# Which engine waits for the last stores and clears their semaphore: GpSimd in place of SyncE

## The chip, the cores and the metric

The kernel runs on one core of one Trainium2 chip. A core has five engines with an instruction stream each: TensorE (not used here), VectorE (DVE in the profile), ScalarE (ACT), GpSimd (POOL) and SyncE (SP, which only issues transfers and handles semaphores). They run in parallel and order their work by semaphores: an instruction may wait until a semaphore has reached a value, and may raise one when it is done. The metric is the device time of one execution in microseconds (us).

## The reference

The input has shape (32, 512, 1024) in float32. For each of the 16,384 rows of 1024 numbers the variance is wanted, as mean of squares less square of the mean:

```python
def reference(x: np.ndarray) -> np.ndarray:
    mean_sq = np.mean(x**2, axis=-1)
    sq_mean = np.mean(x, axis=-1)**2
    return (mean_sq - sq_mean).astype(np.float32)
```

So 64 MiB are read and 64 KiB are written.

## The kernel before

The 16,384 rows are laid out as 128 partitions by 128 columns; a column is one row of 1024 numbers on each partition. The results gather in the tile `mv`, whose second half `mv[:, 1, :]` is what is stored.

SyncE issues all transfers, one after the other. Two buffers `xt0` and `xt1` hold 16 columns each. They are filled and emptied in three turns (96 columns), and the last 32 columns come in eight loads of falling size (`END_LOADS`) and three pieces of one column (`PIECES`), so that little work is left when the last bytes land. `load` (L97) issues a transfer, with a semaphore that rises by 16 when it has landed.

The work on the columns is shared. VectorE takes `BATCH_NORM_STATS2` and an aggregate for most of them (L121, L223 in a loop, L253 to L276 at the end). ScalarE takes the others in two passes, a mean and then squares about it (L125, L130), and one half of the last column but one (L306, L312). GpSimd copies finished results into `mv` (L176) and joins the statistics of 14 of VectorE's columns (L184 to L203); its last instruction is the third L203.

What stands around the change is the end of SyncE's program, L332 to L343. Three stores go out, each from `store` (L106, issued at L108) and each raising `stored` by 16 when it has landed. The first, of 16 columns, waits for the first copy (L332). The second waits for GpSimd's last step, for ScalarE and for VectorE (L334 to L336). The third waits for VectorE's last aggregate, L276 (L338). Then SyncE waits until VectorE has raised `ended` five times (L278, L279, L340) and clears the semaphores of the list `sems` with one instruction (L341). `stored` isn't in that list. For it SyncE waits until it has reached 48, that is until all three stores have landed, and clears it by a second instruction (L342, L343). A wait and the instruction behind it appear as one instruction in the profile.

`sync` is SyncE and `gps` is GpSimd (L82).

Of the kernel before, what the change touches and what calls it, by code (L numbers as in the profile page):

```python
# [11 lines left out]
def kernel(  # L12
# [69 lines left out]
    sync, act, dve, gps = nc.sync, nc.scalar, nc.vector, nc.gpsimd  # L82
# [11 lines left out]
    stored = nc.alloc_semaphore("stored")  # L94
# [244 lines left out]
    store(early, ncols)  # L339
    sync.wait_ge(ended, DVE_END)  # L340
    sync.sem_clear(range(sems[0].num, sems[-1].num + 1))  # L341
    sync.wait_ge(stored, 48)  # L342
    sync.sem_clear(stored)  # L343


# [28 lines left out]
```

## Time and profile before

| what | value |
|---|---|
| median of 3 runs | 162.6 us (162.5 to 162.6) |
| the profiled execution's own time | 162.62 us |
| its span, first to last instruction | 161.3 us |
| VectorE busy | 103.3 us (64%) |
| ScalarE busy | 106.1 us (66%) |
| GpSimd busy | 4.1 us (3%) |
| read from memory | 67.11 MB, 416 GB/s over the span |
| third store, from issue to landing | 1.4 us |

The span runs from the first to the last instruction of the program; what the time has beyond it lies before and behind. The chain of work that ended last is followed back from the last instruction, at each step to what released it. In a row of a waits view stand who waited, for whom, the total in us, how often, and the longest. In a row of one line's view stand engine and operation, the count, the shortest, median and longest duration in ns, and the first and last start in us. A "q" behind an engine's name means that its sequencer did it, the part that waits, branches and issues. Beside the instructions, the trace records each time that a semaphore's value was changed, with the semaphore's number, also after the last instruction of the program.

### The profile page before, as it was taken

The page shows a single profiled execution, that of the slowest core. Times are in us where ns is not written, and L with a number is a line of the kernel's source. Part 1 is how long each engine was busy: PE and PEld are TensorE (multiplying, and loading weights), DVE is VectorE, ACT ScalarE, POOL GpSimd, SP SyncE. Part 2 cuts the span into 40 slices and gives each one's busy share as a digit, 9 for nine tenths or more (in the row PEclk, how much of TensorE's full clock was granted, in tenths as well). Part 3 has the DMA queues.
Part 4 walks back from the last instruction along what each step waited for, and adds up shares of the span by engine and source line. Part 5 has one row for each costly group of instructions (what it writes and reads, how often), then busy time and mean ns, then how long its engine had stood idle before and what let it go on. Part 6 is the DMA issues. An engine that isn't in the chain of part 4 may idle for free. (4 is left out here: it accounts for less than half of the span.)

```text
span 161.3 us, 577 instructions
## 1 busy us (share of the span) xinstructions
DVE 103.3 (64%) x232; ACT 106.1 (66%) x189; POOL 4.1 (3%) x20
## 2 busy tenths in 40 slices
DVE  0000029980499606994089921999139999999896
ACT  3000039972599807996089941999339979999994
POOL 0000000000000000000000000000000000000700
DMA  7969969959959959959959969969969999899993
GB/s 264 520 260 520 520 260 520 520 260 520 520 260 520 520 260 520 520 260 520 520 260 520 520 276 504 520 276 504 520 260 504 406 390 496 360 441 412 425 396 89
DMA packets 2883, 67.20 MB, mean 417 GB/s; under 512 B 704, under 2 KB 960, under 8 KB 1344
## 3 DMA queue, kind: packets, MB, share of 16 engines
q1 hardware_dynamic: 2880, 67.18, 97.3%
q14 instruction: 3, 0.02, 0.1%
HBM read 67.11 MB, written 0.07 MB: 416 GB/s over the span
## 5 line engine op out<-in xcount | busy, mean ns | idle before, releaser
L121 DVE BATCH_NORM_STATS2 stats<-xt 128x6 f32<-128x512 f32 x120 | 71.8, 680 | 54.9 <-DVEq L117 54.9
L125 ACT ACTIVATE junk<-xt 128x1024 bf16<-128x1024 f32 x41 | 42.7, 1043 | 44.1 <-ACTq L117 43.7
L130 ACT ACTIVATE junk_sq<-xt,neg_mean 128x1024 f32<-128x1024 f32 x36 | 39.9, 1107 | 5.6 <-ACTq L117 4.1
L121 DVE BATCH_NORM_STATS2 stats_join<-xt 128x6 f32<-128x512 f32 x22 | 13.1, 684 | 0.0
L125 ACT ACTIVATION_READ_ACCUMULATOR junk<-xt 128x1 f32 x41 | 7.7, 187 | 0.0
L130 ACT ACTIVATION_READ_ACCUMULATOR junk_sq<-xt,neg_mean 128x1 f32 x36 | 6.7, 186 | 0.0
L223 DVE BATCH_NORM_AGGREGATE stage<-stats 128x2 f32<-128x12 f32 x60 | 5.1, 163 | 0.9
L130 ACT ACTIVATE junk_sq<-xt_end,neg_mean_end 128x1024 f32<-128x1024 f32 x5 | 5.5, 1110 | 0.1
L130 ACT ACTIVATE junk_sq<-xt,neg_mean_end 128x1024 f32<-128x1024 f32 x5 | 5.5, 1105 | 0.1
L125 ACT ACTIVATE junk<-xt_end 128x1024 bf16<-128x1024 f32 x5 | 5.2, 1044 | 0.2 <-DMA xt_end<-in_x_dram 0.2
L253 DVE BATCH_NORM_STATS2 stats_end<-xt_end 128x6 f32<-128x512 f32 x6 | 4.1, 685 | 0.7 <-DMA xt_end<-in_x_dram 0.7
L176 POOL COPY mv<-stage 128x32 f32<-128x32 f32 x3 | 0.6, 209 | 130.9 <-ACT junk_sq L130 130.9
L257 DVE BATCH_NORM_STATS2 stats_end<-xt_end 128x6 f32<-128x512 f32 x6 | 3.9, 647 | 0.0
L121 DVE BATCH_NORM_STATS2 stats_join<-xt_end 128x6 f32<-128x512 f32 x6 | 3.7, 696 | 0.0
L281 ACT ACT_TABLE_LOAD x1 | 1.3, 1283 | 2.8 <-PEq L156 2.8
L269 DVE BATCH_NORM_STATS2 stats_end<-xt_end 128x6 f32<-128x256 f32 (+1 forms) x3 | 1.3, 490 | 0.0
L262 DVE BATCH_NORM_AGGREGATE mv<-stats_end 128x2 f32<-128x12 f32 x6 | 1.2, 194 | 0.0
L130 ACT ACTIVATION_READ_ACCUMULATOR junk_sq<-xt,neg_mean_end 128x1 f32 x5 | 0.9, 187 | 0.0
L125 ACT ACTIVATION_READ_ACCUMULATOR junk<-xt_end 128x1 f32 x5 | 0.9, 186 | 0.0
L130 ACT ACTIVATION_READ_ACCUMULATOR junk_sq<-xt_end,neg_mean_end 128x1 f32 x5 | 0.9, 186 | 0.0
L312 ACT ACTIVATE junk_sq<-xt_end,shared 128x512 f32<-128x512 f32 x1 | 0.7, 691 | 0.1
L306 ACT ACTIVATE junk<-xt_end 128x512 bf16<-128x512 f32 x1 | 0.6, 630 | 0.1
(20 smaller groups left out, 5.1 us busy)
## 6 DMA issues: line engine op xcount, KB each, us to landing
xt<-in_x_dram SPq DMA_DIRECT2D x2, 4096.0 KB, 19.1
xt_end<-in_x_dram SPq DMA_DIRECT2D x1, 2560.0 KB, 29.4
xt_end<-in_x_dram SPq DMA_DIRECT2D x1, 2048.0 KB, 33.8
xt_end<-in_x_dram SPq DMA_DIRECT2D x2, 1024.0 KB, 36.8
xt_end<-in_x_dram SPq DMA_DIRECT2D x2, 512.0 KB, 39.0
xt_end<-in_x_dram SPq DMA_DIRECT2D x1, 256.0 KB, 39.6
xt_end<-in_x_dram SPq DMA_DIRECT2D x2, 128.0 KB, 36.0
xt<-in_x_dram SPq DMA_DIRECT2D x6, 24.1
```

Of the source, the lines that this page charges most:

```text
L121: last = dve.bn_stats(out=st[:, h, :], in_=xcol[:, h * H : (h + 1) * H])
L125: return act.activation(out=junk[i], in_=xcol, func=ACTF.Copy, scale=-S / D, accum_out=nm)
L130: return act.activation(out=junk_sq[i], in_=xcol, func=ACTF.Square, scale=S, bias=nm, accum_out=var)
L176: gps.tensor_copy(out=mv[:, 1, t * PER_TURN : (t + 1) * PER_TURN], in_=stage[:, :, 1]).then_inc(copied, 1)
L223: last = dve.bn_aggr(out=stage[:, j, :], in_=stats[:, j, :, :])
L253: dve.bn_stats(out=st[:, 0, :], in_=col[:, :H])
L257: dve.bn_stats(out=st[:, 1, :], in_=col[:, H:]).then_inc(dve_step, 1)
L262: return dve.bn_aggr(out=mv[:, :, c], in_=st)
L269: last = dve.bn_stats(out=st[:, i, :], in_=end_col(c)[:, f : f + size])
L281: act.preload_act_table(ACTF.Square)
L306: act.activation(out=junk[0][:, :H], in_=half, func=ACTF.Copy, scale=1.0 / H, accum_out=shared[:, 0, 1:2],).then_inc(act_step, 1)
L312: act.activation(out=junk_sq[0][:, :H], in_=half, func=ACTF.Square, scale=-1.0, bias=shared[:, 0, 1:2], accum_out=shared[:, 0, 2:3],).then ...
```

## The change

The wait for `stored` and its clearing are given to GpSimd. They come after all else in the text of the program, so on GpSimd they stand behind the last L203. SyncE's program ends with L341.

```diff
     store(early, ncols)
     sync.wait_ge(ended, DVE_END)
     sync.sem_clear(range(sems[0].num, sems[-1].num + 1))
-    sync.wait_ge(stored, 48)
-    sync.sem_clear(stored)
+    gps.wait_ge(stored, 48)
+    gps.sem_clear(stored)
```

## The prediction

> **What bounds the kernel now.** I read the chain of work that ended last, then SyncE's waits, then the rows of the two lines that the change moves, and last the trace's record of semaphore changes, which goes on behind the last instruction. The chain first:
>
> ```profile
> ## 4 chain that ended last, share of the span: by engine, by line
> DMA 21%; DVE 6%; ACT 1%; SPq 1%; issue 0%
> ```
>
> The kernel is bound by the load of 67 MB and then by the statistics of the last columns. VectorE finishes these at 159.81 us, and after that no engine computes. The change touches only what comes after. SyncE's waits show that part:
>
> ```profile
> SPq L108 <- DVE mv L276: 4.7, 1, 4.7
> SPq L343 <- DMA out_dram<-mv: 1.0, 1, 1.0
> ```
>
> The last store is issued when the last aggregate is done, and L343 waits 1.0 us for it to land. The rows of L341 and L343 (duration, start, start):
>
> ```profile
> L341 SPq EVENT_SEMAPHORE_RANGE_CLEAR  x1: 68/68/68, 160.2 to 160.2; - x1
> ...
> L343 SPq EVENT_SEMAPHORE_RANGE_CLEAR  x1: 25/25/25, 161.3 to 161.3; - x1
> ```
>
> L343 is the last instruction of the span. The issue row gives the store's flight, and GpSimd's timeline its last work:
>
> ```profile
> out_dram<-mv SPq DMA_DIRECT2D x1, 3.5 KB, 1.4
> ```
>
> ```profile
> 152.58 0.87 POOL L203 TENSOR_SCALAR mv<-mu 128x6 f32<-128x6 f32 x3
> ```
>
> GpSimd has been done since 153.45 us, so it can stand at a wait 7.8 us ahead of the landing.
>
> The semaphore record tells what follows. The store's last landing is at 161.265 us, and L343 starts at 161.281, clears its semaphore and ends at 161.306. Semaphore 2, which the kernel doesn't use, then changes in a pattern. Its nine changes at the end of this program are at 2.968, 159.261, 159.299, 160.699, 161.438, 161.481, 161.519, 161.554 and 161.600 us. I match them with the engines' last instructions: TensorE's is at 2.68, ScalarE's busy time ends at 159.14, GpSimd's at 153.45, VectorE's last increment starts at 159.96, and SyncE's clear ends at 161.306. So each engine reports when it is done and its predecessor has reported, in the order TensorE, ScalarE, GpSimd, VectorE, SyncE. GpSimd, long done, follows ScalarE by 38 ns. Then the pass goes back through VectorE, GpSimd, ScalarE and TensorE. SyncE is last now, and **from its report to the end of the pass takes 162 ns**. After the pass, from 161.559 on, the semaphores change once more in five blocks of neighbouring numbers. The block that ends last (up to 53) starts after the 161.600 change and ends at 162.165. A second nine-step pass runs from 162.389 to 162.746. The profiled execution took 162.62 us with a span of 161.3, so some 1.3 us lie outside, about as long as this closing from 161.306 to 162.746. The median of the runs shown is 162.6 (162.5 to 162.6), so the profiled one stands for them.
>
> **The change, part by part.** *Removed from SyncE*: one wait and one clear. SyncE is then free at L341's end, 160.29 us, and waits for VectorE's report at 160.70. Nothing that SyncE issues moves: its three stores, with the same waits, stand ahead of both lines, on the same queue. The landing stays at 161.265. The gain is the whole tail between landing and SyncE's report, 161.438 - 161.265 = 173 ns, and it counts only if nothing takes its place.
>
> *Added to GpSimd*: the same wait and the same clear behind L203. Nothing of the kernel is queued behind them on GpSimd, and no instruction waits for them. What waits is the closing pass: VectorE, SyncE and the way back can't go on until GpSimd has reported. No data moves, and no other queue is passed.
>
> The price of GpSimd's tail, from landing to report, by its own rows at the start of the program:
>
> ```profile
> L156 POOLq EVENT_SEMAPHORE  x4: 17/17/17, 2.1 to 2.6; - x4
> ...
> L156 POOLq DRAIN  x3: 34/41/67, 2.0 to 2.5; - x3
> ...
> L156 POOLq EVENT_SEMAPHORE_RANGE_CLEAR  x1: 51/51/51, 2.4 to 2.4; - x1
> ```
>
> A wait there ended 23 ns after its releaser (2.113 to 2.136; SyncE's L343 needed 16). Its clear took 51 ns against 25. Its sequencer started such instructions 78 to 80 ns apart where SyncE needed 60 and 64. From the start of its clear to its report SyncE took 157 ns, which is two such steps and the time of the report itself, some 30. For GpSimd I put two steps of 80, 30 for the report, and 67 for the longest of the three drains, since an engine with work in it may have to be emptied where SyncE has none: 257. With the 23 of the wait that is 280 ns against 173: **+107 ns, taken as 0.10 us.**
>
> The profile does not show GpSimd reporting late, so I bound this. The low end is a report as quick as ScalarE's, 119 ns after its last busy end (159.142 to 159.261). With 23 for the wait and 51 for the clear that is 193 against 173, +0.02 us; SyncE's own 173 would give 0. The high end is VectorE: its last increment starts at 159.959 and its report comes at 160.699, 740 ns later, where two of its steps (93 each) and 30 would be 216. So some 0.52 us of unknown kind lie there. In the present kernel they are hidden beneath the store's flight. On GpSimd they would be bare: 0.10 + 0.52 = +0.62 us. GpSimd has no loop and no branch at its end, which makes it more like SyncE and ScalarE, and I take 0.10.
>
> *Moved*: which engine is the last to report. With SyncE last, 162 ns remain. With GpSimd last the pass must still go up through VectorE and SyncE and come back. The record has this case once: in a nine-step pass before the span's start (from -7.627 to -2.360 us) the third change comes 0.98 us after the second, and from it the steps are 44, 23, 125, 38, 35 and 50 ns, 315 in all. The 125 is VectorE's turn: its second report comes 148 ns after its first there, and 136 and 122 in the two passes where all are ready. Only when SyncE came late, 739 ns after VectorE's first report, did the second follow SyncE's by 43. **So I take 315 - 162 = +0.15 us.** That is the high bound, with the slowest of the three turns. The low one is a VectorE that answers 43 after SyncE: 44 + 23 + 43 + 120 = 230, +0.07.
>
> The Trainium skill, page "Runtime: NRT & Kernel Launch", section "The ~15µs preamble/postamble breakdown", describes such a pass over the five engines with 44 ns for each hop and about 355 ns for all. The trace's full pass took 357 (162.389 to 162.746), so the total agrees, but its steps run from 23 to 125 ns. By an even 44, a late SyncE leaves four hops (176) and a late GpSimd six (264); that is an estimate of +0.09 us in place of 0.15, and the sum by it would be 0.19, or 162.8.
>
> Sum: 0.10 + 0.15 = **+0.25 us**, so 162.62 + 0.25 = 162.87, told as **162.9 us**. No work hides it, since all engines have finished computing by then.
>
> **The rivals.**
>
> *GpSimd's tail has a piece like VectorE's.* For it speaks that VectorE's 0.52 us has no row that explains it, and that GpSimd alone has drains up to 169 ns in the opening. Against it, SyncE and ScalarE report within 132 and 119 ns. Its time: 162.62 + 0.62 + 0.15 = 163.4.
>
> *Not slower: GpSimd reports as early as SyncE did, and the pass is as short.* This is one mechanism: GpSimd stands 7.8 us at its wait, so the steps behind it could be decoded already, and the two steps that SyncE takes, some 130 ns, fall away. Its report would then come 23 + 51 + 30 = 104 ns after the landing, 69 ns ahead of SyncE's. A gain would begin where GpSimd's tail is below 173 - 153 = 20 ns; at 104 the sum is -0.07 + 0.15 = +0.08, so 162.7, and with the low bound of the pass 0.00, so 162.6. Both are within the 0.2% that a measurement of this kernel can tell from no change (0.33 us). A gain of more than 0.33 us can't come from here, because the landing at 161.265 precedes all of it and the removed tail is 0.17 in all. Against it: GpSimd's steps are 80 ns apart even where nothing is awaited.
>
> *Faster, through code places.* One instruction less on SyncE and one more on GpSimd shift where their code blocks end. The record has an 8 KB instruction transfer at 161.14, inside the wait, whose owner it doesn't name. If that transfer was SyncE's and held the closing back, it would now run earlier, and at best the closing's longest unexplained stretch would go, 0.22 us from 161.600 to the first recorded clear of the last block (161.824), with the 0.02 that the removed tail (0.17) leaves over the longer pass (0.15): 162.62 - 0.24 = 162.4, just below the measurable bound only if the landing moves too. Against it, SyncE's report comes 132 ns after L343, with no stall in it.
>
> *The change does nothing*, if GpSimd passes its wait before the landing. The count of 48 needs the last store's 16 increments, of which the last is the 161.265 one, so I leave it a trace of chance, in the not slower case.
>
> **How the numbers follow.** Forecast 0.60: from 162.7 to 163.1, as GpSimd's tail goes from +0.02 to +0.30. VectorE-like tail 0.20: 163.1 to 163.4. Not slower 0.15: 162.6 to 162.7. Faster 0.05. The bound of 0.2% lies at 162.93, inside the forecast's own range and little above its centre. Since what I may have left out of GpSimd's tail only adds, I put 0.33 of the forecast's 0.60 above it and 0.27 below. Slower: 0.33 + 0.20 = 0.53. Within: 0.27 + 0.15 = 0.42. Faster: 0.05. The range goes from 162.6, below which is the faster case, to 163.4, the high bound.
>
> **What would show it.** In the changed profile the span's last instruction is GpSimd's clear, its row near 50 ns and its start within 30 ns of the last landing; SyncE's last row is L341, ended near 160.3; SyncE's wait for the store is gone, and GpSimd has one of some 8 us. The span itself grows by 0.03 us only, so most of the loss must lie outside it: the third change of semaphore 2 some 280 ns after the landing and the ninth 315 after that. The forecast is wrong if the last landing moves by over 0.2 us, if the third change comes within 150 or after 500 ns, or if the pass from there takes 162.

## The result, and the profile after

The changed kernel is slower: 163.27 us (median of 7 runs, 163.1 to 163.61) against 162.73 us for the kernel before beside it (median of 7, 162.5 to 163.06). The ratio is 1.0036, with a 95% interval from 1.0026 to 1.0046, so about 0.6 us (0.42 to 0.75). The profiled execution took 163.14 us, 0.52 more than that of before.

The chain of work and SyncE's waits of the changed kernel:

```profile
DMA 21%; DVE 6%; SPq 1%; ACT 1%; issue 0%
```

```profile
SPq L108 <- DVE mv L276: 4.7, 1, 4.7
SPq L358 <- PEq L358: 0.7, 1, 0.7
```

Every computing group stands as it did, within 0.1 us of busy time, and SyncE's wait for the store is gone from the list. The wait of some 8 us that was forecast for GpSimd has no row in the waits view; it follows from the end of L203 (153.44) and the start of the clear (161.258), 7.8 us later. The rows of the two clears, of the store and of GpSimd's last computation:

```profile
L341 SPq EVENT_SEMAPHORE_RANGE_CLEAR  x1: 67/67/67, 160.2 to 160.2; - x1
```

```profile
L343 POOLq EVENT_SEMAPHORE_RANGE_CLEAR  x1: 44/44/44, 161.3 to 161.3; - x1
```

```profile
out_dram<-mv SPq DMA_DIRECT2D x1, 3.5 KB, 1.4
```

```profile
152.56 0.88 POOL L203 TENSOR_SCALAR mv<-mu 128x6 f32<-128x6 f32 x3
```

SyncE now ends with L341, and GpSimd's clear is the last instruction of the span, at the same 161.3 us. The span is 161.3 us as before. **Nothing in the span shows the loss; all of it lies behind the last instruction.** It is in the record of semaphore changes. Nine changes of semaphore 2 close the program, and the engine that waits for the stores is the one whose report holds the pass up:

| us from the span's start | before | after |
|---|---|---|
| last landing of the third store | 161.265 | 161.234 |
| start of the clear (L343) | 161.281 (SyncE) | 161.258 (GpSimd) |
| the waiting engine's report | 161.438 (fifth change) | 161.829 (third change) |
| ninth change | 161.600 | 162.115 |
| ninth change of the next pass | 162.746 | 163.264 |

From landing to report it was 173 ns and is 595. From the report to the end of the pass it was 162 ns and is 286. Together that is 335 and 881 ns, or 0.546 us more. The landing came 31 ns earlier, so 0.515 us of it is left at the end of the pass, 0.518 at the end of the next pass, and 0.52 in the time.

### The profile page after: what moved, and what is told of

Read it like the earlier page. It is cut to its first block, busy times and chain, and to the rows that moved or that the text cites. A ratio compares the mean times of both kernels' runs of the same rounds, so it can differ in the third digit from the quotient of the medians.

```text
span 161.3 us, 577 instructions
## 1 busy us (share of the span) xinstructions
DVE 103.4 (64%) x232; ACT 106.1 (66%) x189; POOL 4.1 (3%) x20
```

## The experiments

In all of them I read three numbers from the semaphore record: the tail (from the store's last landing to the report of the engine that waits for it), the way back (from that report to the ninth change) and the profiled time less the landing. The landing itself moved from 161.16 to 161.68 us from one profiled execution to another, which hides effects of 0.1 us in the times but not in these.

| run | who waits | tail, ns | way back, ns | sum, ns | time less landing, us | ratio to before (95%) |
|---|---|---|---|---|---|---|
| before | SyncE | 173 | 162 | 335 | 1.355 | |
| after | GpSimd | 595 | 286 | 881 | 1.906 | 1.0036 (1.0026 to 1.0046) |
| e1_pad16 | GpSimd | 596 | 286 | 882 | 1.901 | 1.0036 (1.0025 to 1.0048) |
| e2_pad64 | GpSimd | 601 | 285 | 886 | 1.903 | 1.0036 (1.0020 to 1.0051) |
| e3_early | SyncE | 173 | 165 | 338 | 1.360 | 0.9997 (0.9988 to 1.0007) |
| e4_act | ScalarE | 186 | 325 | 511 | 1.533 | 1.0014 (1.0002 to 1.0025) |
| e5_sync_late | SyncE | 596 | 164 | 760 | 1.776 | 1.0020 (1.0008 to 1.0032) |
| e6_dve | VectorE | 235 | 242 | 477 | 1.503 | 1.0010 (1.0000 to 1.0020) |
| e7_pe | TensorE | 326 | 360 | 686 | 1.707 | 1.0022 (1.0012 to 1.0031) |
| e8_no_library | GpSimd | 595 | 287 | 882 | 1.901 | 1.0042 (1.0025 to 1.0059) |
| e9_drain | GpSimd | 655 | 287 | 942 | 1.966 | 1.0032 (1.0021 to 1.0043) |
| e10_no_clear | SyncE | 160 | 165 | 325 | 1.342 | 0.9995 (0.9986 to 1.0004) |

**Time less landing is the sum plus 1.02 us in every row (1.016 to 1.026).** So the two terms add up, and nothing else behind the landing changed the time in any of the runs.

**Is GpSimd's tail a place in its code, or its own work?** After the change GpSimd reports 571 ns after the start of its clear (161.258 to 161.829). The theories were that a costly slot lies right behind its last instruction (A), or that GpSimd has closing work (B). Two kernels put more instructions ahead of the wait, as `pad` in the diff:

```diff
+    for _ in range(16):
+        gps.sem_inc(pad, 1)
     gps.wait_ge(stored, 48)
-    gps.sem_clear(stored)
+    gps.sem_clear(range(stored.num, pad.num + 1))
```

> The changed kernel with 16 semaphore increments on GpSimd between its last computation and its wait (some 80 ns each, from 153.5 to 154.7 us, so they end long before the landing); its clear covers their semaphore too. In the changed kernel GpSimd's report (the third of nine closing changes of semaphore 2) comes 571 ns after the start of its clear, where SyncE's came 157 after its own. Theory A, a place in the code: some slot right behind GpSimd's last instruction costs the extra 0.4 us, as at the end of a code block. Then 16 instructions more move that slot in front of the wait, the report comes 200 to 280 ns after the clear, and the time falls by 0.3 to 0.4 us to about 0.2 us over the kernel before. Theory B, GpSimd's own closing work: 571 stays within 40 ns and the time stays 0.5 us over the kernel before.

> The same with 64 increments (some 5.1 us, to 158.6 us, still before the landing). Theory A: if the costly slot lies further back than 16, it is in front of the wait here; the report comes 200 to 280 ns after the clear, time about 0.2 us over the kernel before. If it was cured by 16 it stays cured unless another block ends there. Theory B: the report stays at 571 ns within 40, time 0.5 us over the kernel before.

The padding in e2_pad64, by its line's view:

```profile
L344 POOLq EVENT_SEMAPHORE  x64: 17/17/17, 153.3 to 158.5; - x64
```

It ran where it should, long before the landing. With 16 and with 64 increments the clear started at 161.404 and 161.331 us, and the report came at 161.975 and 161.908: 571 and 577 ns. With 64, an 8 KB instruction transfer appeared at 158.466 that no other run has, so it is likely that the padding made GpSimd load one more piece of code, and the tail stayed all the same. A has fallen for GpSimd.

The next kernel takes the landing out of it. SyncE waits for the stores as before; GpSimd waits for VectorE's fifth increment, which gets a semaphore of its own:

```diff
-    DVE_END = 5
+    DVE_END = 4
...
+    dve.sem_inc(extra, 1)
...
     sync.wait_ge(stored, 48)
     sync.sem_clear(stored)
+    gps.wait_ge(extra, 1)
+    gps.sem_clear(extra)
```

> The kernel before, where SyncE waits for the stores, and GpSimd with a wait and a clear of its own, released not by a landing but by VectorE's fifth increment at about 159.96 us. GpSimd has nothing of the path, so the time is that of the kernel before within 0.1 us under every theory. Theory B (GpSimd's own closing work): its report comes 570 ns within 40 after the start of its clear, near 160.55. Theory C, that the landing of the store or the instruction transfer at 161.13 holds GpSimd up in the changed kernel: the report comes 200 to 280 ns after the clear, near 160.2. Theory A gives the same as B here, as the code ends nearly at the same place.

```profile
L347 POOLq EVENT_SEMAPHORE_RANGE_CLEAR  x1: 44/44/44, 160.3 to 160.3; - x1
```

The clear started at 160.273, 1.2 us before the last store had landed (161.520), and the report came at 160.843: 570 ns. So the landing does not hold GpSimd up, and the instruction transfer (161.420 here) doesn't either: no such transfer is recorded between this clear and this report. This kernel has the same closing work as the changed one, and it costs nothing: SyncE reports at 161.693, and GpSimd's 570 ns lie beneath the store's flight. In the kernel before they would have been over by 154.1, as GpSimd had been done since 153.45, long before ScalarE's report at 159.261.

What GpSimd's extra 0.4 us are (571 ns where SyncE took 157) was the next question. One guess was the pool configuration that the trace shows ahead of GpSimd's arithmetic in the changed kernel:

```profile
L184 POOLq MODIFY_POOL_CONFIG  x2: 13/13/13, 134.3 to 134.3; - x2
```

```diff
     steps = [
-        lambda: gps.tensor_tensor(out=two, in0=mean[:, :, 0:2], in1=mean[:, :, 2:4], op=ALU.add),
...
+        lambda: gps.tensor_copy(out=mu, in_=mean[:, :, 0:1]) for _ in range(9)
     ]
```

> The changed kernel with GpSimd's twelve steps (L184 to L203) replaced by plain copies, so the variances of the 14 columns that they join are left out. The two pool configuration instructions that stand ahead of L184 in the trace (134.3 us) then go. Theory B1: GpSimd's closing work of 0.4 us undoes that configuration; without it the report comes 200 to 280 ns after the clear, time 0.2 us or less over the kernel before. Theory B2: it is there in any case; 571 ns within 40, time 0.5 us over the kernel before.

With copies alone the configuration is gone from the trace:

```profile
149.68 2.31 POOL L184 COPY mu<-stats_join 128x14 f32<-128x14 f32 x9 [15.00 <-DVE stats_join L121]
```

From the start of the clear (161.583) to the report (162.154) it is 571 ns again. The other guess was the emptying of the engine, so a drain was set behind the clear:

```diff
     gps.sem_clear(stored)
+    gps.drain()
```

> The changed kernel with a drain on GpSimd behind its clear. If GpSimd's extra 0.4 us is the first emptying of the engine after its work, the drain's row shows it (300 ns or more, where the drains of the opening took 34 to 169) and the report stays near 570 to 650 ns after the clear. If it is something that the closing does whatever stands before, the drain takes under 100 ns and the report moves back by its step of 80 ns, to about 650: drain short, 490 to 570 still left behind it.

```profile
L344 POOLq DRAIN  x1: 34/34/34, 161.8 to 161.8; - x1
```

The drain took 34 ns, and the report came 631 ns after the start of the clear, 60 later than without it. So the extra time is not what a drain does, and a drain in front doesn't take it away; the closing does something on GpSimd in each of these kernels. **What it does is still open**: no instruction is recorded between the clear and the report. Shown is that it takes 570 to 577 ns from the start of the clear in the five runs that end with it (after, e1, e2, e3 and e8), and that it moves back when GpSimd's program ends later.

**Is the longer way back a term of its own?** For this SyncE got the tail that GpSimd has:

```diff
     sync.wait_ge(stored, 48)
-    sync.sem_clear(stored)
+    for _ in range(7):
+        sync.sem_inc(pad, 1)
+    sync.sem_clear(range(stored.num, pad.num + 1))
```

> The kernel before, with seven semaphore increments on SyncE between the wait for the stores and the clear (60 to 64 ns each by SyncE's steps, 0.42 to 0.45 us in all). This gives SyncE about the tail that GpSimd has in the changed kernel (595 ns from landing to report, 422 more than SyncE's 173) without moving the last report to GpSimd. If tail and way back add up as two terms: report 0.60 us after the landing, from it to the ninth change 162 ns, time 0.42 to 0.45 us over the kernel before and 0.12 under the changed one (whose way back takes 286). If the time ends with something else than the ninth change, it stays near the kernel before.

```profile
L345 SPq EVENT_SEMAPHORE  x7: 17/17/17, 161.2 to 161.5; - x7
...
L346 SPq EVENT_SEMAPHORE_RANGE_CLEAR  x1: 31/31/31, 161.6 to 161.6; - x1
```

The tail was 596 ns, that of the changed kernel within 1, and the way back 164. Time less landing is 1.776, which is 0.421 over the kernel before and 0.130 under the changed one. The loss is thus 0.42 for the tail and 0.12 for the way back. The ratio, 1.0020 (0.13 to 0.52 us), holds this.

**The other engines.** The same two lines were given to ScalarE, VectorE and TensorE:

```diff
-    gps.wait_ge(stored, 48)
-    gps.sem_clear(stored)
+    act.wait_ge(stored, 48)
+    act.sem_clear(stored)
```

> ScalarE waits for the stores and clears their semaphore in place of GpSimd. Its report is the second of the nine. Theory B (the 0.4 us are GpSimd's): the report comes within 150 to 250 ns of the landing; from it the pass takes 38+44+23+98+38+35+47 = 323 ns by the steps of the second closing pass, 161 more than with SyncE; time 0.16 to 0.25 us over the kernel before, less than with GpSimd by 0.3. A theory that any engine other than SyncE pays 0.57 us after such a wait: report 0.57 us after the clear, time 0.55 to 0.6 over the kernel before.

> VectorE waits for the stores and clears their semaphore. Theory B for VectorE (its 740 ns from last instruction to report are closing work of its own, whatever stands before): report some 740 ns after the start of the clear, the way back from it 23+98+38+35+47 = 241 ns, time (760 - 173) + (241 - 162) = 0.67 us over the kernel before. Theory A for VectorE (the extra 0.52 us are a code place that its last increments pass, with the instruction transfer at 161.13 as its trace): the wait now stands behind that place, report 200 to 280 ns after the clear, time 0.12 to 0.2 us over the kernel before.

> TensorE, which computes nothing here, waits for the stores and clears their semaphore; its report is the first of nine, so the whole pass follows it: 357 ns. If a plain engine's tail is 150 to 250 ns (SyncE 173, ScalarE 186): time 0.17 to 0.28 us over the kernel before. If TensorE has closing work like GpSimd: 0.6 us or more over it.

```profile
L343 ACTq EVENT_SEMAPHORE_RANGE_CLEAR  x1: 41/41/41, 161.2 to 161.2; - x1
```

```profile
L343 DVEq EVENT_SEMAPHORE_RANGE_CLEAR  x1: 61/61/61, 161.4 to 161.4; - x1
```

```profile
L343 PEldq EVENT_SEMAPHORE_RANGE_CLEAR  x1: 63/63/63, 161.6 to 161.6; - x1
```

The clears alone explain little of it (25 ns on SyncE, 63 on TensorE). ScalarE reported 165 ns after the start of its clear, VectorE 208 and TensorE 298. The two expectations for ScalarE's pass and VectorE's held within 2 ns (325 for 323, 242 for 241). TensorE's tail, 326, is longer than the 150 to 250 of a plain engine and half of GpSimd's, between the two theories; its cost of 0.352 us is as large because the whole pass follows it (198 ns more than follow SyncE). VectorE took 739 to 741 ns from its last increment to its report in the four kernels in which its report was held up by nothing else (before, e3, e5 and e10). In e6 that did not come back: the report came 208 ns after the start of the clear, as theory A had it in size. The extra 0.52 us are passed while VectorE stands at the wait, so they are not closing work behind whatever comes last, as GpSimd's are. What they are is open. The instruction transfer that the expectation took for their trace can't be their cause: in the kernel before it starts at 161.140, 0.44 us after VectorE's report. Nor does it keep its place behind VectorE's last increment, with 1.18 to 1.21 us in eleven kernels and 1.42 in e10.

**Can the clear be left out?** The last kernel keeps SyncE's wait and drops the clear:

```diff
     sync.wait_ge(stored, 48)
-    sync.sem_clear(stored)
```

> The kernel before without the clear of the stores' semaphore: SyncE only waits. The closing clears that semaphore in any case (it changes once more at 161.743 us). If the two steps from the wait to the report stay, only the clear's 25 ns against a wait's 17 are saved: time as before within 0.1 us. If the clear costs a step of its own, the report comes some 62 ns earlier: 0.06 us under the kernel before, which 0.2% can't tell; the semaphore record can.

```profile
L342 SPq EVENT_SEMAPHORE  x1: 17/17/17, 161.6 to 161.6; - x1
```

The tail was 160 ns for 173. That is 13 ns by the record and nothing by the time (0.9986 to 1.0004), so the clear costs no step of its own, which would have been some 62 ns. No kernel here beats the one before by what can be measured.

## Why the prediction was right or wrong

*Right: where the path goes.* That the change touches only what follows the last landing, that the landing stays, that the span grows by nothing that matters and the loss lies outside it, and that the closing pass waits for GpSimd in third place, all came as the record of before had it. The order of the engines that was read from their last instructions has been confirmed by moving the wait to each of the five: the late report was the first change for TensorE, the second for ScalarE, the third for GpSimd, the fourth for VectorE and the fifth for SyncE.

*Right, a little too large: the way back.* Forecast +0.15 with bounds 0.07 and 0.15; measured 286 - 162 = +0.124. The size of the earlier pass, 315, was taken with its slowest turn of VectorE (148 ns after its first report); here that turn took 121 (161.873 to 161.994). The estimate of 0.09 by the even 44 ns a hop of the Trainium skill (page "Runtime: NRT & Kernel Launch", section "The ~15µs preamble/postamble breakdown") was a little farther off. The steps of 23 to 125 ns that the prediction set against it come from two passes: in the one that took 357 they run from 24 to 98.

*Wrong in size: GpSimd's tail.* The step that failed is the 280 ns put together from two steps of 80, a report, the longest drain, and the wait. It measured 595. The wait and the clear were right (24 ns to the start for 23, and 44 for 51); the rest was not the sum of sequencer steps. The forecast had said that it would be wrong with a third change later than 500 ns after the landing, and so it was. The sum of the forecast was +0.25 us and the measured one +0.546 by the record. The time stayed inside the range only because that range reached to a GpSimd with an unexplained piece: 163.14 us lies above the forecast's own 162.7 to 163.1, in the band that was given a chance of 0.20.

*The rivals.* That piece was there, and the rival that put one there named 0.52 us on the model of VectorE. It measured 595 - 280 = 315 ns beyond the forecast's own tail, about six tenths of that, so the rival's 163.4 was too high where the forecast's 162.9 was too low. Its model fell: VectorE's piece vanishes when VectorE waits, and GpSimd's doesn't. The bound was borrowed from an engine whose cost has another nature. That GpSimd landed near it is in part luck. The choice of SyncE and ScalarE as the engines that GpSimd is most like, for want of a loop at its end, was the wrong reading. The pass ahead of the span, where GpSimd's report came 0.98 us after ScalarE's, would not have given the size either: in the other runs that gap goes from 0.21 to 1.30 us, and what sets it is not shown. Nor are long drains GpSimd's alone, as the rival had it: SyncE has one of 128 ns in the opening. The rival that GpSimd has its steps decoded ahead, with a report at 104 ns, fell with the 595. The one of the code places fell with the time: the instruction transfer starts at 161.126 where it was at 161.140, and the stretch of 0.22 us behind the ninth change is there as before (162.115 to 162.335). That the wait would be passed before the landing did not happen: L343 started 24 ns after it.

## What to carry to other kernels

By these runs the last wait of a kernel belongs to the engine for which the time to its report and the way back from it are shortest together; in this kernel that was SyncE, whose report the pass needs last (335 ns in all, against 477 to 881 for the others). An idle engine isn't a free one: what GpSimd does at its end was hidden only as long as another engine ended later. A profile's span ends with the last instruction, so a loss behind it is to be sought in the semaphore record and in the time less the span.

## What the runs showed of the hardware that had not been expected

- GpSimd needed 570 to 577 ns from the start of its last clear to its report, in five kernels with different code before it, where SyncE needed 148 to 157, ScalarE 165, VectorE 208 and TensorE 298.
- What the time has beyond landing, tail and way back is fixed: 1.016 to 1.026 us in all twelve profiled kernels.
- The moment of the last landing varies by 0.5 us (161.16 to 161.68) between profiled executions of kernels that do much the same up to it. Only the change to GpSimd, 0.546 us, costs as much; the other three moves cost 0.15 to 0.35 by the record.
